# The MLPs' inner activations: transposed by transposing DMA transfers of 16-bit halves instead of by TensorE

## The chip, the cores and the metric

The kernel runs on one core of a Trainium2 chip. The metric is the time of one execution on the device, in microseconds (us); the median of three runs of the kernel before is 2459.45 us (2459.42 to 2463.46).

## The reference

A decoder trunk of two layers for 256 tokens with 2048 features, all in float32. Layer 0 is a retention layer, layer 1 multi-head latent attention; each is followed by an MLP with a squared ReLU and an inner width of 8192:

```
def sq_relu_mlp(h, w1, w2):
    return jnp.square(jax.nn.relu(h @ w1)) @ w2
...
for layer in range(DEPTH):
    ...
    x = x + sq_relu_mlp(rms_norm(x, norm_mlp[layer]), mlp_w1[layer], mlp_w2[layer])
```

The change concerns what happens between the two products of each MLP.

## The kernel before, in words

Activations stand on 128 partitions. A product needs its left operand with the features on the partitions (feature-major), and gives its result with the tokens on the partitions (token-major), 128 tokens in each of two tiles. So the result of `h @ w1` has to be turned before it can be the left operand of the product with `w2`.

Float32 precision is made of three products of a reduced format: each operand is split into a high part and a low part (`split`, line 213: ScalarE casts the high part, VectorE subtracts it for the low part), and `mm` (line 405) issues high times high, high times low and low times high.

**Weights.** `quad` (line 321) takes a megabyte of weights, issued from SP's queue into one of three `raw` buffers, and splits it into high and low parts (`wh`, `wl`, five buffers each). A plain quad has 8 block products, 24 matmuls. In a "seven" quad sums of weight blocks are formed by VectorE first (lines 363 to 373), and 7 block products, 21 matmuls, are enough. `gemm_pair` (line 386) runs eight quads over 1024 result columns and gathers them in four to eight PSUM banks; `pair_out` (line 427) copies the banks out with ScalarE and VectorE combines the sevens' results.

**The MLP.** `mlp` (line 864) goes in four groups. A group has two pieces of `h @ w1` (here u_0 and u_1, named after the count of the piece, p) and two pieces of the product with `w2` (d_00 and d_01: group and piece). Quad k of piece u_1 is u_1k, of piece d_00 it is d_00k. So in each of the two layers four groups of four pieces of eight quads follow each other.

**Between the products.** When a piece u_p has ended, `up` (line 871) runs inside the next piece: it finishes the sums, applies the ReLU with the scale of the norm (ScalarE, line 877), and calls `turn` twice. Each `turn` (line 879) handles 512 columns: for two blocks of 256 columns TensorE transposes four tiles of 128x128 into a PSUM bank (`transposed`, line 230, matmul against the identity at line 235), ScalarE squares from PSUM into SBUF (line 886), `split_act` splits the result, and for the odd blocks `with_sums` (line 451) prepares the sums that sevens need. A piece d_g0 takes its blocks in order: d_004 to d_007 need what u_1 gave, which is turned during d_000 to d_003.

**Order.** Nothing runs ahead of its place in an engine's queue: each engine executes in order. The program is written quad by quad; work between the products is put off by `later` (line 97), which counts in quads, and `tick` runs what is due. A scheduler then merges the work into each engine's queue, so that the order on an engine is not quite the order of the text. Temporaries come from one pool (`f2k`, 14 buffers).

## Time and profile before

| | |
|---|---|
| median of three runs | 2459.45 us |
| span of the profiled execution | 2456.3 us |
| TensorE (PE) busy | 2446.2 us |
| VectorE (DVE) busy | 2212.2 us |
| ScalarE (ACT) busy | 1641.3 us |
| first matmul of the first MLP (u_0), first of d_00 | 721.3 us, 808.6 us from the start |
| last matmul of the second MLP | about 2451 us |
| transposes of the inner activations | 256, 272 ns each |

The time that the profiled execution itself took is not listed beside its span; the medians stand for it. In the rows, PE is TensorE, DVE VectorE, ACT ScalarE, POOL GpSimd and SPq the queue of SyncE, which issues the transfers of weights. A row of the timeline gives the start, the time, the engine, the line, the operation, what it writes and reads, and in brackets the idle time before it and what ended it. "x3" joins instructions in a row, whose times then overlap. Layer numbers and buffer numbers are cut from the names (u_wh, d_raw, hid_u). In the chain of waits a piece is the time from one release to the next.

### The profile page before, as it was taken

To read this page: it belongs to the slowest core of one execution; us is meant where nothing else is said; L and a number is where in the kernel's file an instruction comes from. 1 tells how busy PE (TensorE), PEld (TensorE's weight loads), DVE (VectorE), ACT (ScalarE), POOL (GpSimd) and SP (SyncE) were. 2 spreads that over 40 slices of the span, in tenths; PEclk is the share of its full clock that TensorE was granted. 3 is DMA by queue.
4 is the path that set the end of the run, shared out by engine and by line. 5 is a ranking of instruction groups with operands and counts; after the bars stand their busy time and mean duration, and the time that the engine had idled before them with its cause. 6 is when DMAs were issued, how large, how long until landed. Compare 5 with 4: busy or idle time off the path is not lost.

```text
span 2456.3 us, 31721 instructions
## 1 busy us (share of the span) xinstructions
PE 2446.2 (100%) x11614; PEld 2057.6 (84%) x11614; DVE 2212.2 (90%) x2919; ACT 1641.3 (67%) x2307; POOL 238.0 (10%) x287
## 2 busy tenths in 40 slices
PE   9999999999999999999999999999999999999999
PEld 7888888888888888888888888998888888888887
DVE  7899899888899999999999998777899999999998
ACT  6566666556676767667676777577667667676674
POOL 6400001000000010010110001101000100100100
PEclk9999999999999999999999999999999999999999
DMA  8555569556565586695786555444555865957854
GB/s 309 207 201 191 192 202 259 191 183 224 197 218 194 196 254 218 207 272 187 241 253 213 200 202 180 155 162 173 197 199 205 252 228 194 262 198 229 264 209 170
DMA packets 93692, 521.05 MB, mean 212 GB/s; under 512 B 11104, under 2 KB 12512, under 8 KB 40288
## 3 DMA queue, kind: packets, MB, share of 16 engines
q1 hardware_dynamic: 72144, 472.83, 55.2%
q0 software_dynamic: 21248, 46.15, 8.9%
q8 instruction: 91, 1.49, 0.2%
q14 instruction: 65, 0.53, 0.1%
q10 hardware_dynamic: 144, 0.05, 0.0%
HBM read 479.14 MB, written 39.85 MB: 211 GB/s over the span
## 4 chain that ended last, share of the span: by engine, by line
PE 92%; DVE 2%; ACT 1%; issue 0%; DMA 0%; POOL 0%; ACTq 0%; DVEq 0%
PE u_c L411 7%; PE u_c L410 7%; PE u_c L409 7%; PE d_c L411 6%; PE d_c L410 6%; PE d_c L409 6%; PE rp_c L411 3%; PE rp_c L409 3%; PE rp_c L410 3%; PE u_p L411 2%; PE u_p L410 2%; PE u_p L409 2%; PE rq_acc L307 2%; PE rk_acc L307 2%; PE ro_c L411 2%; PE ro_c L409 2%
## 5 line engine op out<-in xcount | busy, mean ns | idle before, releaser
L217 DVE TENSOR_TENSOR d_wl<-d_raw,d_wh 128x1024 fp32r<-128x1024 f32 (+1 forms) x256 | 278.7, 1111 | 31.6 <-ACT d_wh L216 31.6
L217 DVE TENSOR_TENSOR u_wl<-u_raw,u_wh 128x1024 fp32r<-128x1024 f32 (+1 forms) x256 | 279.3, 1113 | 29.8 <-ACT u_wh L216 29.8
L409 PE MATMUL u_c<-u_wh,n 128*128 128x512 f32 x712 | 278.3, 392 | 0.0
L411 PE MATMUL u_c<-u_wh,n 128*128 128x512 f32 x712 | 277.2, 389 | 0.0
L410 PE MATMUL u_c<-u_wl,n 128*128 128x512 f32 x712 | 277.2, 389 | 0.0
L409 PE MATMUL d_c<-d_wh,hid 128*128 128x512 f32 x706 | 275.4, 392 | 0.5 <-ACT d_wh L216 0.5
L411 PE MATMUL d_c<-d_wh,hid 128*128 128x512 f32 x706 | 275.0, 390 | 0.0
L410 PE MATMUL d_c<-d_wl,hid 128*128 128x512 f32 x706 | 274.8, 389 | 0.0
L216 ACT CAST u_wh<-u_raw 128x1024 fp32r<-128x1024 f32 (+1 forms) x256 | 241.3, 973 | 49.6 <-PE u_c L411 24.1
L216 ACT CAST d_wh<-d_raw 128x1024 fp32r<-128x1024 f32 (+1 forms) x256 | 240.3, 971 | 39.9 <-PE d_c L411 16.6
L216 ACT CAST d_wh<-d_u 128x1024 fp32r<-128x1024 f32 x106 | 108.1, 1051 | 119.7 <-DVE d_u L373 82.6
L216 ACT CAST u_wh<-u_u 128x1024 fp32r<-128x1024 f32 x104 | 106.2, 1052 | 116.0 <-DVE u_u L373 77.3
L411 PEld LDWEIGHTS u_c<-u_wh,n 128*128 128x128 f32 x712 | 133.7, 188 | 27.8
L410 PEld LDWEIGHTS u_c<-u_wl,n 128*128 128x128 f32 x712 | 133.8, 188 | 27.4 <-DVE u_wl L217 0.3
L409 PEld LDWEIGHTS u_c<-u_wh,n 128*128 128x128 f32 x712 | 133.7, 188 | 27.0
L409 PEld LDWEIGHTS d_c<-d_wh,hid 128*128 128x128 f32 x706 | 132.6, 188 | 28.2 <-ACT d_wh L216 1.4
L411 PEld LDWEIGHTS d_c<-d_wh,hid 128*128 128x128 f32 x706 | 132.5, 188 | 27.6
L410 PEld LDWEIGHTS d_c<-d_wl,hid 128*128 128x128 f32 x706 | 132.6, 188 | 27.5 <-DVE d_wl L217 0.4
L216 ACT CAST rp_wh<-rp_raw 128x1024 fp32r<-128x1024 f32 x112 | 103.8, 945 | 74.2 <-PE rp_c L411 49.2
L217 DVE TENSOR_TENSOR rp_wl<-rp_raw,rp_wh 128x1024 fp32r<-128x1024 f32 x112 | 119.7, 1090 | 16.4 <-ACT rp_wh L216 16.2
L217 DVE TENSOR_TENSOR u_wl<-u_u,u_wh 128x1024 fp32r<-128x1024 f32 x104 | 123.5, 1222 | 3.1 <-ACT u_wh L216 2.8
L217 DVE TENSOR_TENSOR d_wl<-d_u,d_wh 128x1024 fp32r<-128x1024 f32 x106 | 125.8, 1221 | 0.0
(570 smaller groups left out, 6505.3 us busy)
## 6 DMA issues: line engine op xcount, KB each, us to landing
u_raw<-in_mlp_w SPq DMA_DIRECT2D x128, 1024.0 KB, 5.4
d_raw<-in_mlp_w SPq DMA_DIRECT2D x128, 1024.0 KB, 4.9
rp_raw<-in_ret_w_gv SPq DMA_DIRECT2D x56, 1024.0 KB, 4.8
ro_raw<-in_ret_w_out SPq DMA_DIRECT2D x32, 1024.0 KB, 4.9
uq_raw<-in_mla_w_uq SPq DMA_DIRECT2D x24, 768.0 KB, 4.3
rq_raw<-in_ret_w_qk SPq DMA_DIRECT2D x16, 1024.0 KB, 4.9
rk_raw<-in_ret_w_qk SPq DMA_DIRECT2D x16, 1024.0 KB, 4.8
xh<-d_c POOLq DMA_DIRECT2D x48, 256.0 KB, 6.1
```

What stands on the lines that cost most here:

```text
L216: nc.scalar.copy(h, src)
L217: return nc.vector.tensor_tensor(l, src, h.bitcast(F32), op=ALU.subtract)
L307: nc.tensor.matmul(acc[f], wh[:, cols], a.rearrange("p i s -> p (i s)"), start=k == 0, stop=k == nk - 1)
L409: nc.tensor.matmul(dst, ah, bh, start=n == 0, stop=False)
L410: nc.tensor.matmul(dst, ah, bl, start=False, stop=False)
L411: nc.tensor.matmul(dst, al, bh, start=False, stop=n == total[key] - 1)
```

## The change

The transposes of `turn` leave TensorE. A float32 word is seen as two 16-bit halves (`halves_of`). After the ReLU, ScalarE copies each tile of 512 columns into two planes, one with the first and one with the second halves (`turn_by_dma`, two copies of 1024 halves for the two token tiles). Two or three quads later SP issues four transposing transfers, one for each token tile and plane, from SBUF to SBUF, 128 partitions x 512 halves (128 KB) each. Then ScalarE joins the planes: for each block of 256 columns it copies the two turned planes of 512 halves into the alternate halves of `u` (`joined`), squares `u` in place, and goes on as before with `split_act` and `with_sums`. The transposing transfers stand in the same queue as the weights' loads.

```diff
+    def halves_of(v):
+        return v.bitcast(U16).rearrange("p (n two) -> p two n", two=2)
+
+    def turn_by_dma(blocks, name, wait, steps, then):
+
+        parts = [f2k([2, 512], f"{name}_h{t}", U16) for t in range(NT)]
+        for t in range(NT):
+            nc.scalar.copy(parts[t], halves_of(blocks[t]))
+
+        def turn():
+            turned = [f2k([4, S], f"{name}_t{i}", U16) for i in range(2)]
+            for t in range(NT):
+                for i in range(2):
+                    nc.sync.dma_start_transpose(turned[i][:, :, t * P : (t + 1) * P], parts[t][:, i])
+            for k2 in range(2):
+                later(steps[k2], lambda k2=k2: then(turned, k2))
+
+        later(wait, turn)
+
+    def joined(turned, k2, u):
+
+        for i in range(2):
+            dst = halves_of(u.rearrange("p j s -> p (j s)"))[:, i]
+            nc.scalar.copy(dst, turned[i][:, 2 * k2 : 2 * k2 + 2].rearrange("p j s -> p (j s)"))
...
                 c = summed(c)
-                for t in range(NT):
-                    for i in range(2):
+
+                def turn(i):
+                    for t in range(NT):
                         nc.scalar.activation(c[t][i], c[t][i], AF.Relu, scale=r[t])
-
-                def turn(i):
-                    for q in (2 * i, 2 * i + 1):
-                        name = f"hid{layer}_{p}{q}"
-                        tp = transposed(
-                            lambda t, j: c[t][q // 2][:, (q % 2 * 2 + j) * P : (q % 2 * 2 + j + 1) * P], f"{name}_tp"
-                        )
-                        u = f2k([2, S], f"{name}_u")
-                        nc.scalar.activation(u, tp, AF.Square)
-                        v = act_tile(name)
-                        split_act(v, u)
-                        blocks.append((v, with_sums(u, name) if len(blocks) in ODD else None))
-                        hid.append(v)
+                    wait = 3 if p % 2 == 0 or i else 2
+                    turn_by_dma(
+                        [c[t][i] for t in range(NT)], f"hid{layer}_{p}{i}", wait, (0, 1),
+                        lambda turned, k2: square(turned, i, k2),
+                    )
+
+                def square(turned, i, k2):
+                    name = f"hid{layer}_{p}{2 * i + k2}"
+                    u = f2k([2, S], f"{name}_u")
+                    joined(turned, k2, u)
+                    nc.scalar.activation(u, u, AF.Square)
+                    v = act_tile(name)
+                    split_act(v, u)
+                    blocks.append((v, with_sums(u, name) if len(blocks) in ODD else None))
```

How the change moves instructions is shown at three places, all at the beginning of piece d_00. The lines of the changed kernel are numbered higher (L213 to L217 became L214 to L218, L363 became L389, L455 became L481).

On VectorE, as d_00 begins: the low parts of its first weights (d_000_wl, d_001_wl) and the sums of piece u_1 (u_1_c, u_1_v, u_1_u, u_1_p). Before:

```order
L217 TENSOR_TENSOR d_000_wl_7401<-d_000_raw,d_000_wh_7400 128x1024
L217 TENSOR_TENSOR d_000_wl_7421<-d_000_raw,d_000_wh_7420 128x1024
L448 TENSOR_TENSOR u_1_c_7386<-u_1_c_7386,u_1_p_7390 128x512
L434 TENSOR_TENSOR u_1_v<-u_1_p_7211,u_1_p_7390 128x512
L435 TENSOR_TENSOR u_1_u<-u_1_p_7211,u_1_v 128x512
L217 TENSOR_TENSOR d_001_wl_7476<-d_001_raw,d_001_wh_7475 128x1024
L438 TENSOR_TENSOR u_1_v<-u_1_p_7392,u_1_v 128x512
L448 TENSOR_TENSOR u_1_c_7388<-u_1_c_7388,u_1_u 128x512
```

And now:

```order
L218 TENSOR_TENSOR d_000_wl_7409<-d_000_raw,d_000_wh_7408 128x1024
L474 TENSOR_TENSOR u_1_c_7394<-u_1_c_7394,u_1_p_7398 128x512
L460 TENSOR_TENSOR u_1_v<-u_1_p_7165,u_1_p_7398 128x512
L461 TENSOR_TENSOR u_1_u<-u_1_p_7165,u_1_v 128x512
L218 TENSOR_TENSOR d_000_wl_7429<-d_000_raw,d_000_wh_7428 128x1024
L464 TENSOR_TENSOR u_1_v<-u_1_p_7400,u_1_v 128x512
L474 TENSOR_TENSOR u_1_c_7396<-u_1_c_7396,u_1_u 128x512
L465 TENSOR_TENSOR u_1_p_7400<-u_1_p_7400,u_1_u 128x512
L474 TENSOR_TENSOR u_1_c_7392<-u_1_c_7392,u_1_v 128x512
L474 TENSOR_TENSOR u_1_c_7390<-u_1_c_7390,u_1_p_7400 128x512
L218 TENSOR_TENSOR d_001_wl_7459<-d_001_raw,d_001_wh_7458 128x1024
```

The second low part of d_000 has moved behind three of the sums, and the first low part of d_001 behind all eight.

On ScalarE, from quad d_003 to quad d_004, now: casts of weights (d_003_wh, d_004_wh), and the joins (L262) of the turned planes (hid_10_t) into hid_10_u and hid_11_u. Before, the casts of d_003 and d_004 follow each other with one cast of hid_13_more between them.

```order
L217 CAST d_003_wh_7579<-d_003_u_7545 128x1024
L262 COPY hid_10_u<-hid_10_t_7530 128x512
L262 COPY hid_10_u<-hid_10_t_7531 128x512
L262 COPY hid_11_u<-hid_10_t_7530 128x512
L915 ACTIVATE hid_10_u<-hid_10_u 128x512
L262 COPY hid_11_u<-hid_10_t_7531 128x512
L217 CAST hid_10_7540<-hid_10_u 128x2x256
L915 ACTIVATE hid_11_u<-hid_11_u 128x512
L217 CAST d_004_wh_7606<-d_004_raw 128x1024
```

The work on the first two blocks of u_1 now stands directly ahead of the first cast of d_004, whose matmuls are the first that need them.

On SP's queue, now, from the load of d_004 on (hid_10_h are the planes, hid_10_t what the transfers write):

```order
L350 DMA d_004_raw<-in_mlp_w_0 128x2048
L252 DMA_TRANSPOSE hid_10_t_7530<-hid_10_h_7452 128x4x128
L252 DMA_TRANSPOSE hid_10_t_7531<-hid_10_h_7452 128x4x128
L252 DMA_TRANSPOSE hid_10_t_7530<-hid_10_h_7453 128x4x128
L252 DMA_TRANSPOSE hid_10_t_7531<-hid_10_h_7453 128x4x128
L350 DMA d_005_raw<-in_mlp_w_0 128x2048
L350 DMA d_006_raw<-in_mlp_w_0 128x2048
L252 DMA_TRANSPOSE hid_11_t_7638<-hid_11_h_7492 128x4x128
```

Before, the loads of d_004 to d_007 follow each other there. Now the first four transfers stand between the loads of d_004 and d_005, and the other four between those of d_006 and d_007.

More of the change, by code (lines that the diff above doesn't have):

```diff
@@ L15 @@
 I32 = mybir.dt.int32
+U16 = mybir.dt.uint16
 AF = mybir.ActivationFunctionType
```

4 lines of the change are left out of this document (2 added, 2 removed).

## The prediction

> **What bounds the kernel now.** The page's first part and its chain of waits come first.
>
> ```profile
> span 2456.3 us, 31721 instructions
> PE 2446.2 (100%) x11614; PEld 2057.6 (84%) x11614; DVE 2212.2 (90%) x2919; ACT 1641.3 (67%) x2307; POOL 238.0 (10%) x287
> ...
> PE 92%; DVE 2%; ACT 1%; issue 0%; DMA 0%; POOL 0%; ACTq 0%; DVEq 0%
> ```
>
> TensorE works in all of the span, and the chain runs through it for 92%. So whatever leaves TensorE's queue is a gain until another engine is late. Which one is next is read by stage: busy time in four stretches of the first MLP (u_1, d_00, d_01 and the stretch after).
>
> ```profile
> core 0: us, PE busy (x) PEld busy (x) DVE busy (x) ACT busy (x) POOL busy (x), PEclk, DMA share, GB/s
> 765.00:808.00 43.00, 43.00 (x200) 35.77 (x199) 40.65 (x52) 31.32 (x43) 0.00 (x0) 1.00 0.57 196
> 808.00:852.00 44.00, 44.00 (x204) 36.62 (x203) 41.86 (x53) 32.31 (x45) 0.00 (x0) 1.00 0.55 192
> 852.00:895.00 43.00, 43.00 (x192) 35.61 (x191) 39.69 (x45) 27.29 (x33) 7.82 (x9) 1.00 0.87 248
> 895.00:938.00 43.00, 43.00 (x191) 35.65 (x190) 39.22 (x44) 28.13 (x33) 6.03 (x7) 1.00 0.91 265
> ```
>
> The first two stretches hold the transposes; VectorE is busy there for 40.65 of 43 and 41.86 of 44 us, about 95%, ScalarE for 73%, and the clock is granted in full. What VectorE does not change, TensorE cannot outrun by much. In the last two VectorE has 92%: there a lag can be worked off.
>
> **What is removed.** The view of a tile gives the number of transposes, the chain in order of time what a run of eight costs, and the timeline TensorE's step.
>
> ```profile
> L235 PE MATMUL hid_tp<-cst,u_c x256: 270/272/273, 770.8 to 2378.3; 128*128 128x128 f32 x128
> ```
> ```profile
> 770.95 0.87 PE hid_tp L235 x8
> ...
> 814.23 0.87 PE hid_tp L235 x8
> ```
> ```profile
> 803.87 0.39 PE L409 MATMUL u_p<-u_wh,n 128*128 128x512 f32 x1
> ...
> 808.17 0.39 PE L410 MATMUL u_p<-u_wl,n_more 128*128 128x512 f32 x1
> ```
>
> One transpose lasts 272 ns, but they overlap: eight take 0.87 us of the chain. 256 of them are 32 runs, so 32 x 0.87 = 27.8 us leave TensorE. That is the ceiling: 2459.45 - 27.8 = 2431.6 us. (The execution shown has a span of 2456.3 us; the 3.1 us up to the median of the runs lie outside what the change touches, so differences are taken from the median.) A matmul of 512 columns starts 0.2265 us after the one before (19 steps in 4.30 us); a quad of 24 takes 5.44 us, a seven of 21 takes 4.76.
>
> **What ScalarE gains in work.** Rows of its timeline in u_1 and at the start of d_00:
>
> ```profile
> 765.55 1.09 ACT L216 CAST u_wh<-u_raw 128x1024 fp32r<-128x1024 f32 x1
> ```
> ```profile
> 804.07 0.59 ACT L432 COPY u_c<-u_c 128x512 f32<-128x512 f32 x1 [1.61 <-PE u_c L411]
> 804.55 1.05 ACT L216 CAST d_wh<-d_raw 128x1024 fp32r<-128x1024 f32 x1
> ...
> 806.93 1.08 ACT L432 COPY u_c<-u_c 128x512 f32<-128x512 f32 x2
> ...
> 810.41 2.98 ACT L216 CAST d_wh<-d_raw 128x1024 fp32r<-128x1024 f32 x3
> 813.24 2.22 ACT L877 ACTIVATE u_c<-u_c,n_r 128x512 f32<-128x512 f32 x3
> ```
>
> Queued behind each other, 1024 elements take 0.95 us, a copy of 512 takes 0.48, a Relu 0.63 (overlapped starts). Each turn adds two copies of 1024 halves and four joins of 512: 2 x 0.95 + 4 x 0.48 = 3.8 us; the Square stays. Two turns fall into a stretch such as 765 to 808: 31.3 + 7.6 = 38.9 us of the 41.3 that TensorE would then need. It fits, if a copy of every second half costs what a plain copy does. No row shows one. From below nothing, since elements are counted alike; from above twice, since it touches every second word.
>
> **What the queue of SP gains.** 128 transposing transfers of 128 KB, eight per pair of turns. No row shows one. The nearest are plain transfers, in the view of the DMA queues and issues, in SP's timeline and in its waits:
>
> ```profile
> q1 hardware_dynamic: 72144, 472.83, 55.2%
> q0 software_dynamic: 21248, 46.15, 8.9%
> ```
> ```profile
> d_raw<-in_mlp_w SPq DMA_DIRECT2D x128, 1024.0 KB, 4.9
> ...
> dec<-in_decay SPq DMA_DIRECT2D x8, 128.0 KB, 4.9
> ...
> x0t<-in_xt SPq DMA_DIRECT2D x2, 128.0 KB, 2.9
> ```
> ```profile
> 772.58 0.33 SPq L324 DMA_DIRECT2D u_raw<-in_mlp_w  x1
> ```
> ```profile
> 815.85 0.33 SPq L324 DMA_DIRECT2D d_raw<-in_mlp_w  x1
> ```
> ```profile
> 819.90 0.33 SPq L324 DMA_DIRECT2D d_raw<-in_mlp_w  x1
> ```
> ```profile
> SPq L324 <- DVE d_wl L217: 592.7, 122, 7.6
> ```
>
> On SP's queue a megabyte keeps the 16 engines for 55.2% of 2456.3 / 472.83 = 2.87 us, on GpSimd's smaller pieces for 4.74; for 128 KB (0.131 MB) that is 0.38 to 0.62 us in a stream. The far end is 2.9 us, a 128 KB transfer alone from issue to landing, if the four of a turn go one after another. I take 0.5, between the two queues, because the four stand in one queue behind a load like a stream. Engines have the room: eight are 4 us, and in 43 us they are idle for 43%. SP itself issues a plain transfer in 0.33 us and otherwise waits for VectorE to let go of raw buffers (122 waits, 592.7 us). In the new order four transfers stand behind d_004's load; what is queued behind them is d_005's load, whose buffer is free only 4 us after d_004's (815.85 and 819.90). So they delay no load if each is issued within 1 us.
>
> [...]
>
> **Where it is late.** I follow one pair of turns by hand, on the clock of the profile; VectorE's rows carry it.
>
> ```profile
> 801.51 2.35 DVE L217 TENSOR_TENSOR u_wl<-u_u,u_wh 128x1024 fp32r<-128x1024 f32 x2
> ```
> ```profile
> 805.63 1.23 DVE L217 TENSOR_TENSOR d_wl<-d_raw,d_wh 128x1024 fp32r<-128x1024 f32 x1 [1.76 <-ACT d_wh L216]
> ...
> 811.60 0.69 DVE L438 TENSOR_TENSOR u_v<-u_p,u_v 128x512 f32<-128x512 f32 x1
> 812.20 0.68 DVE L448 TENSOR_TENSOR u_c<-u_c,u_u 128x512 f32<-128x512 f32 x1
> ...
> 814.60 2.36 DVE L217 TENSOR_TENSOR d_wl<-d_raw,d_wh 128x1024 fp32r<-128x1024 f32 x2
> 816.87 0.42 DVE L455 TENSOR_TENSOR hid_sum<-hid_u 128x256 f32<-128x256 f32 x1
> ...
> 818.41 0.29 DVE L456 TENSOR_TENSOR hid_sum<-hid_sum,hid_u 128x128 f32<-128x128 f32 x1
> 818.61 1.22 DVE L217 TENSOR_TENSOR d_wl<-d_raw,d_wh 128x1024 fp32r<-128x1024 f32 x1
> ```
>
> In a queue, 1024 elements take VectorE 1.13 us (the last of a run 1.23), 512 take 0.60, 256 take 0.34, 128 take 0.20.
>
> In u_1, the load of u_14 issues at 772.6 and lands 4.9 later, the four transfers at about 779.6. ScalarE has by then run up against the first join: from u_11's first cast at 765.55 it has ten items of 1024 (that one, five casts, four copies of halves), four Relus and one item of 512 queued, 765.55 + 9.5 + 2.5 + 0.5 = 778.1. So 1.5 us are lost; then join, cast of u_13, join, Square, join, hid cast, cast of u_14: 779.6 + 0.95 + 5 x 0.48 + 1.06 = 784.0, and VectorE's low part of u_14 ends at 785.1. From there to u_17's first low part its queue holds eight passes of 1024 and the last of 1.23, ten of 512, two of 256 and four of 128: 9.04 + 1.23 + 6.0 + 0.68 + 0.8 = 17.7 us, so 802.8. TensorE, two runs (1.74) earlier than 803.87, asks for it at its second matmul, 802.13 + 0.23 = 802.4. **Late: about 0.5 us.**
>
> In d_00 TensorE then starts at 802.13 + 0.5 + 4.76 = 807.4. ScalarE casts u_17's sums, which VectorE ends at 801.7, until 803.8; four copies and a cast later its copy of p1 ends at 807.2, and three sums of VectorE at 809.05. By the new order d_000's second low part follows (810.2), five sums (813.2) and only then d_001's first low part: 814.4. TensorE wants it at 807.4 + 5.44 + 0.23 = 813.1. **Late: 1.3 us.** With that TensorE is back at its old clock (d_001 at 814.1; d_004 at 829.8). d_004's load issues when d_001's low part is done, 815.5, lands at 820.4, the four transfers at 822.4. ScalarE reaches the first join at 823.6 (there are five high-part buffers, and the cast before takes the one that TensorE uses until 822.7): no wait, 1.2 us to spare. Seven items of 0.48 and a cast later, at 828.1, d_004's cast is done, its low part at 829.3, in time for 830.0. From there to d_006's first low part VectorE has five passes of 1024, the last of 1.23, seven of 512 and one of 256 queued, 11.4 us: 840.7, wanted at 839.97 + 0.23 = 840.2. **Late: 0.5**, and to d_007's another 5.7 us (two of 1024, one of 1.23, three of 512, two of 128), 846.4, wanted at 846.1: **late 0.3**.
>
> **The sum.** A group of four pieces has two turns in u_1 and two in d_00: 4 x 0.87 = 3.5 us off, 0.5 + 1.3 + 0.5 + 0.3 = 2.6 back, 0.9 kept. Two layers of four groups: 8 x 0.9 = 7 us. 2459.45 - 7 = **2452 us**. An error of 1 us in a group is 8 us in the time; the forecast's own range is 2444 to 2461.
>
> **The rivals.**
>
> *All of it is kept.* The low parts are in time, as VectorE's lead of about 3 us (it ends u_17's low parts at 803.9, TensorE uses the last from 807.3) swallows the lateness. For it: no stretch exceeds VectorE's time. Against it: 95% busy there, and VectorE idle 1.76 us at the head of each piece for ScalarE, which waits for TensorE. 2432 to 2444 us, say 2437.
>
> *The transfers land after their joins (slower).* The place is d_00: ScalarE is in order, so a join that waits holds up the weights' casts behind it, and with them VectorE and TensorE. Above 0.5 + 1.2 / 4 = 0.8 us per transfer the joins of d_00 wait; each of the 16 transfers of a group then costs what it has above 0.8. The 0.9 us kept are gone at 0.86 us per transfer: from there on it is slower. At 1.0 us it loses 16 x 0.2 = 3.2 us a group, 8 x 3.2 = 26 in all: 2478 us. For it: both queues' packets are longer than the rows of a transpose, and 0.8 is near to 0.62.
>
> *Each transfer waits for the one before.* At 2.9 us, 16 x 2.1 x 8 = 269 us: 2721 us. Against it: loads of one queue overlap in these rows. [...]
>
> *ScalarE's half copies cost twice.* Then 31.3 + 15.2 = 46.5 us against 41.5 in 16 stretches: 5 x 16 = 80, 2532 us. Against it: a cast and a copy take ScalarE equally long per element in the rows.
>
> **The numbers.** A measurement of this kernel tells a difference of about 0.2% (5 us) from none. Forecast 0.43 (0.28 of it below 2454.5, 0.15 within); all kept 0.20; late landing 0.27 (0.04 within); one after another 0.05; double copies 0.05. So faster 0.48, same 0.19, slower 0.33. The range leaves out the last two and the tail of late landings above 1.05 us, and the best of the second: 2433 to 2486.
>
> **What the profile would show.** Right: no hid_tp rows, a PE span shorter by 5 to 10 us; idle time of PE before d_c and u_c that ends with VectorE's low part, 2 to 3 us in a group; ScalarE at about 73%; joins that wait little for the transfers. If TensorE has no such idle time, all is kept; if ScalarE's joins wait for DMA, the transfers are late; if L246 and L262 take twice 0.95 and 0.48, the copies are the cost. Wrong in its ground would be a TensorE that waits for raw weights, since I let the transfers delay no load.

## The result and the profile after

| | median us | change |
|---|---|---|
| before | 2459.43 | |
| after | 2501.12 (2500.70 to 2503.62) | ratio 1.0167 [1.0153, 1.0181] |

It is slower by 41.7 us. The forecast was 2452, faster, in a range of 2433 to 2486: the sign was wrong and the time lies outside the range. The profiled execution of after took 2501.51 us. The head of its page, its chain and its queue:

```profile
span 2499.7 us, 31622 instructions
PE 2447.4 (98%) x11358; PEld 2023.3 (81%) x11358; DVE 2219.1 (89%) x2919; ACT 1765.5 (71%) x2499; POOL 239.5 (10%) x287
...
q1 hardware_dynamic: 141776, 489.62, 59.6%
...
PE 64%; DVE 15%; ACT 10%; DMA 5%; issue 4%; SPq 1%; POOL 0%; ACTq 0%; DVEq 0%
```

The 256 transposes are gone from TensorE, but a third of the chain now runs through other engines. What TensorE waits for is in its waits (total us, times, longest):

```profile
PE d_c L435 <- ACT d_wh L217: 14.4, 17, 2.9
PE d_c L436 <- DVE d_wl L218: 10.5, 17, 1.5
PE u_c L436 <- DVE u_wl L218: 8.5, 10, 0.9
PE u_p L436 <- DVE u_wl L218: 3.6, 11, 0.6
PE d_p L436 <- DVE d_wl L218: 2.6, 8, 0.3
...
PE u_c L435 <- ACT u_wh L217: 1.5, 2, 0.7
```

These are 41.1 us in 65 waits; before, d_c had 0.5 and the others no row. Its timeline shows that a wait costs more than its bracket:

```profile
795.85 0.40 PE L435 MATMUL u_c<-u_wh,n 128*128 128x512 f32 x1
797.12 0.50 PE L436 MATMUL u_c<-u_wl,n 128*128 128x512 f32 x1 [0.87 <-DVE u_wl L218]
797.46 0.40 PE L437 MATMUL u_c<-u_wh,n 128*128 128x512 f32 x1
...
806.17 0.50 PE L436 MATMUL u_p<-u_wl,n 128*128 128x512 f32 x1 [0.36 <-DVE u_wl L218]
...
817.82 0.50 PE L436 MATMUL d_c<-d_wl,hid 128*128 128x512 f32 x1 [0.66 <-DVE d_wl L218]
...
839.02 0.50 PE L436 MATMUL d_p<-d_wl,hid 128*128 128x512 f32 x1 [0.33 <-DVE d_wl L218]
...
852.14 0.50 PE L435 MATMUL d_c<-d_wh,hid 128*128 128x512 f32 x1 [0.45 <-ACT d_wh L217]
...
863.98 0.50 PE L435 MATMUL d_c<-d_wh,hid 128*128 128x512 f32 x1 [0.96 <-ACT d_wh L217]
```

Counted by matmuls from the start of a pair (a plain quad has 24, a seven 21), these six waits are in quads u_15, u_17, d_001, d_005, d_007 and, already in d_01, d_011. The step to 797.12 is 1.27 us instead of 0.2265, 1.04 late where the bracket says 0.87, and the next step is 0.34. So each wait costs some 0.27 more: 41.1 + 65 x 0.27 = 58.7, less the 27.8 removed, is an estimate of 31 of the 41.7 us. The rest lies in longer steps without a row of their own.

**Where it sits.** The starts of the pieces give it by pairs, from the first matmul of one pair to that of the next (before: 84.08 us a pair, 87.3 for the first of a layer). The eight pairs of u together take 9.95 us longer. So do, by 20.94, the six pairs of d that a pair of u follows directly; the last pair of d of each layer, read with the stage behind it, adds 6.9 and 3.8, and 1.8 lie ahead of the first MLP. All below is told in the first two sums, "u" and "d".

**Why TensorE waits** is read on the engines that feed it. VectorE's waits after, and those of the same kind before:

```profile
DVE u_wl L218 <- ACT u_wh L217: 51.2, 45, 4.5
DVE hid L218 <- ACT hid L217: 37.7, 25, 3.5
...
DVE d_wl L218 <- ACT d_wh L217: 7.2, 14, 0.7
```
```profile
DVE u_wl L217 <- ACT u_wh L216: 32.7, 30, 1.8
DVE d_wl L217 <- ACT d_wh L216: 31.6, 28, 1.8
```
```profile
L217 DVE TENSOR_TENSOR hid<-hid_u,hid 128x512 fp32r<-128x512 f32 x64 | 41.4, 690 | 0.0
```

The three kinds are 96.1 us against 64.3 (hid had none before, as its group in the third fence shows: busy time, mean of one, idle time). VectorE, 95% busy in these pieces before, does not get back what it loses: by the page its busy time rose by 6.9 us and its idle time by 36.5, which is the whole 43.4 by which the span grew. It waits for ScalarE, and this is what ScalarE does there:

```profile
781.52 0.77 ACT L262 COPY hid_u<-hid_t 128x512 uint16<-128x512 uint16 x1 [1.19 <-DMA hid_t<-hid_h]
...
826.40 2.03 ACT L262 COPY hid_u<-hid_t 128x512 uint16<-128x512 uint16 x3
828.30 0.62 ACT L915 ACTIVATE hid_u<-hid_u 128x512 f32<-128x512 f32 x1
828.83 0.75 ACT L262 COPY hid_u<-hid_t 128x512 uint16<-128x512 uint16 x1
829.45 0.61 ACT L217 CAST hid<-hid_u 128x512 fp32r<-128x512 f32 x1
...
836.08 1.41 ACT L262 COPY hid_u<-hid_t 128x512 uint16<-128x512 uint16 x2 [1.62 <-DMA hid_t<-hid_h]
```
```profile
830.09 0.69 DVE L218 TENSOR_TENSOR hid<-hid_u,hid 128x512 fp32r<-128x512 f32 x1 [2.32 <-ACT hid L217]
```

Two things are to be seen. At 826.40 nothing waits for a transfer: three joins, a Square, a join and a cast stand behind each other, and VectorE (second fence) is idle for 2.32 us until the cast is done. At 781.52 and 836.08 ScalarE itself is idle, for a transfer that has not landed. The first is order, the second lateness, and the experiments take them apart.

### The profile page after: what moved, and what is told of

It is laid out like the page before. It is cut to its first block, busy times and chain, and to the rows that moved or that the text cites. A ratio compares the mean times of both kernels' runs of the same rounds, so it can differ in the third digit from the quotient of the medians.

```text
span 2499.7 us, 31622 instructions
## 1 busy us (share of the span) xinstructions
PE 2447.4 (98%) x11358; PEld 2023.3 (81%) x11358; DVE 2219.1 (89%) x2919; ACT 1765.5 (71%) x2499; POOL 239.5 (10%) x287
## 3 DMA queue, kind: packets, MB, share of 16 engines
q1 hardware_dynamic: 141776, 489.62, 59.6%
## 4 chain that ended last, share of the span: by engine, by line
PE 64%; DVE 15%; ACT 10%; DMA 5%; issue 4%; SPq 1%; POOL 0%; ACTq 0%; DVEq 0%
PE u_c L436 4%; PE u_c L437 4%; PE u_c L435 4%; DVE d_wl L218 4%; DMA hid_t<-hid_h 3%; PE d_c L436 3%; PE d_c L437 3%; PE d_c L435 3%; PE rp_c L435 2%; PE rp_c L437 2%; PE rp_c L436 2%; PE rq_acc L333 2%; PE rk_acc L333 2%; ACT u_wh L217 2%; DVE u_wl L218 2%
## 5 line engine op out<-in xcount | busy, mean ns | idle before, releaser
L218 DVE TENSOR_TENSOR u_wl<-u_raw,u_wh 128x1024 fp32r<-128x1024 f32 (+1 forms) x256 | 277.4, 1110 | 31.5 <-ACT u_wh L217 30.8
L218 DVE TENSOR_TENSOR d_wl<-d_raw,d_wh 128x1024 fp32r<-128x1024 f32 (+1 forms) x256 | 276.4, 1107 | 6.6 <-ACT d_wh L217 6.2
L437 PE MATMUL d_c<-d_wh,hid 128*128 128x512 f32 x706 | 275.4, 390 | 0.0
L435 PE MATMUL d_c<-d_wh,hid 128*128 128x512 f32 x706 | 259.8, 392 | 14.4 <-ACT d_wh L217 14.4
L217 ACT CAST u_wh<-u_raw 128x1024 fp32r<-128x1024 f32 (+1 forms) x256 | 242.8, 971 | 37.8 <-PE u_c L437 18.0
L217 ACT CAST d_wh<-d_raw 128x1024 fp32r<-128x1024 f32 (+1 forms) x256 | 238.2, 972 | 26.5 <-DMA d_raw<-in_mlp_w 15.8
L217 ACT CAST d_wh<-d_u 128x1024 fp32r<-128x1024 f32 x106 | 107.4, 1051 | 107.7 <-DVE d_u L399 82.8
L217 ACT CAST u_wh<-u_u 128x1024 fp32r<-128x1024 f32 x104 | 106.8, 1050 | 88.0 <-DVE u_u L399 59.5
L217 ACT CAST rp_wh<-rp_raw 128x1024 fp32r<-128x1024 f32 x112 | 103.8, 944 | 74.6 <-PE rp_c L437 49.7
L218 DVE TENSOR_TENSOR u_wl<-u_u,u_wh 128x1024 fp32r<-128x1024 f32 x104 | 123.2, 1218 | 20.7 <-ACT u_wh L217 20.4
L218 DVE TENSOR_TENSOR rp_wl<-rp_raw,rp_wh 128x1024 fp32r<-128x1024 f32 x112 | 119.3, 1086 | 16.9 <-ACT rp_wh L217 16.8
L218 DVE TENSOR_TENSOR d_wl<-d_u,d_wh 128x1024 fp32r<-128x1024 f32 x106 | 124.8, 1217 | 1.1 <-ACT d_wh L217 1.0
```

Source lines behind the costliest of these rows:

```text
L217: nc.scalar.copy(h, src)
L218: return nc.vector.tensor_tensor(l, src, h.bitcast(F32), op=ALU.subtract)
L435: nc.tensor.matmul(dst, ah, bh, start=n == 0, stop=False)
L437: nc.tensor.matmul(dst, al, bh, start=False, stop=n == total[key] - 1)
```

## The experiments

The expectations call the explanations by letters. Theory A: the transfers land late because of their own price, as the rival in the prediction had it. Rival B: ScalarE's added copies and the new order are the loss, whatever the transfers do. Rival C: the order alone that the scheduler laid out around the transfers is the loss. Theory D: what costs is the transfers' place in a queue, behind a weight load and ahead of the next, whatever their price.

All times, with the 95% interval of the ratio to before and the two sums (changes in us against before). A sum is read from the profiled execution, whose own time is up to 3.7 us from the median:

| kernel | us | ratio | u | d |
|---|---|---|---|---|
| after | 2501.12 | [1.0153, 1.0181] | +9.95 | +20.94 |
| no_transfer | 2452.69 | [0.9957, 0.9980] | -9.35 | -1.57 |
| plain | 2472.08 | [1.0033, 1.0063] | -0.74 | +5.44 |
| tensor_plus_transfers | 2459.93 | [0.9987, 1.0006] | 0 | 0 |
| even_by_dma | 2471.38 | [1.0032, 1.0062] | +6.63 | +2.02 |
| no_transfer_order | 2473.75 | [1.0042, 1.0076] | -7.86 | +14.10 |
| plain_order | 2497.50 | [1.0139, 1.0169] | +12.37 | +17.74 |
| plain_rows_order | 2496.09 | [1.0136, 1.0166] | +9.44 | +19.21 |
| early_transfers | 2500.54 | [1.0153, 1.0184] | +29.77 | +5.96 |
| nt_order_ahead | 2467.89 | [1.0022, 1.0046] | +5.43 | -0.44 |
| ahead_order | 2489.42 | [1.0106, 1.0137] | +7.54 | +13.92 |
| even_queued_12 | 2490.32 | [1.0109, 1.0143] | +23.47 | +4.63 |
| even_queued_sp | 2469.19 | [1.0024, 1.0046] | +1.09 | +4.68 |
| full_order | 2471.98 | [1.0034, 1.0063] | -3.47 | +9.33 |
| tensor_same_places | 2459.46 | [0.9988, 1.0007] | 0 | 0 |
| plain_pool_order | 2477.44 | [1.0057, 1.0087] | -5.51 | +14.08 |
| no_transfer_pool | 2489.47 | [1.0102, 1.0136] | +8.94 | +13.16 |
| pool_joins | 2513.27 | [1.0206, 1.0237] | +17.25 | +22.87 |
| after_d1 | 2501.24 | [1.0151, 1.0179] | +12.20 | +22.64 |

### Taking the transfers away, and adding them where nobody waits

no_transfer: the transfers go, the joins read the half copies.

```diff
-                    nc.sync.dma_start_transpose(turned[i][:, :, t * P : (t + 1) * P], parts[t][:, i])
...
-            nc.scalar.copy(dst, turned[i][:, 2 * k2 : 2 * k2 + 2].rearrange("p j s -> p (j s)"))
+            nc.scalar.copy(dst, turned[k2][:, i])
```

> No transfers at all: the joins read the half copies directly (the turning is left out). ScalarE keeps all of its added work. Theory A: nothing is late but what ScalarE and VectorE make late themselves, so 2437 to 2455 us, not above the kernel with plain transfers. Rival B: 2490 to 2500 us, since ScalarE has the same 16 copies per pair of turns.

tensor_plus_transfers: before, with 128 transposing transfers that nobody reads.

```diff
+                def extra(i):
...
+                            nc.sync.dma_start_transpose(
+                                turned[h][:, :, t * P : (t + 1) * P],
+                                c[t][i].bitcast(U16)[:, h * 512 : (h + 1) * 512],
+                            )
...
+                    later(3 if p % 2 == 0 or i else 2, lambda: extra(i))
```

> The kernel before, with TensorE's transposes kept, and the 128 transposing transfers added at the places they have in the changed kernel; nobody reads what they write (the output is as before). No instruction of ScalarE, VectorE or TensorE is added or moved. Theory A splits: what the transfers do by holding SP (a weight load behind them issued up to 5 us later) shows here, without the joins that wait: 2465 to 2490 us if the late loads are the larger half of the loss, 2459 to 2465 if the late joins are. Rival B: 2459 us, as before.

plain: the same pieces moved without turning.

```diff
-                    nc.sync.dma_start_transpose(turned[i][:, :, t * P : (t + 1) * P], parts[t][:, i])
+                    nc.sync.dma_start(turned[i][:, :, t * P : (t + 1) * P], parts[t][:, i].rearrange("p (j n) -> p j n", j=4))
```

> Each transposing transfer of the changed kernel is replaced by a plain transfer of the same 128 KB between the same tiles on the same queue (the activations stay unturned: that part of the computation is left out). Theory A (the price of the transposing transfers: SP held 1.31 us by each, 1.05 us of the 16 engines' time, joins and weight loads late behind them): SP is held about 0.33 us per transfer, the joins no longer wait, and the time falls from 2501 to what was forecast blind, 2444 to 2461 us. Rival B (ScalarE's added copies and the new order on VectorE cost it, whatever the transfers do): it stays at 2490 to 2501 us.

even_by_dma: only the first piece of a pair is turned by transfers, the second by TensorE as before.

```diff
                 def turn(i):
+                    if p % 2 == 1:
+                        return by_tensor(i)
```

> Only the first piece of each pair, whose turns run beside the second u piece, is turned by transfers; the second, whose turns run beside the first d piece, by TensorE as before. 16 runs of TensorE's transposes leave, 13.9 us. In the changed kernel the u pairs took about as long as before, with their 1.74 us each given back, and the d pairs lost 3.4 us. Theory A: so no loss is left and a part of the 13.9 us may stay: 2452 to 2462 us. Rival B: half of ScalarE's added work stays, half the loss: about 2480 us.

Without transfers the time is 2452.69, with ScalarE's added work in it, and the pairs are 1.2 (u) and 0.3 us (d) shorter. So ScalarE's copies by themselves are not the loss; rival B asked for 2490 to 2500 here. That the time is the forecast's own number is chance, for the forecast had transfers in it. With transfers that nobody reads, nothing is lost, although two loads stand behind eight of them, as SP's timeline shows:

```profile
773.84 4.41 SPq L325 DMA_DIRECT2D u_raw<-in_mlp_w  x2
778.31 10.65 SPq L884 DMA_TRANSPOSE x_t<-u_c  x8
789.06 1.09 SPq L325 DMA_DIRECT2D u_raw<-in_mlp_w  x2
```

The last two loads are issued from 789.06 on, where before all four were out in one run from 772.58 to 788.89. So neither the engines' time nor a late load alone is the price, while ScalarE and VectorE keep their old work. plain in its own order is 29 us faster than after, but the scheduler gave it another order, so that this comparison has two causes in it; at 2472.08 it lies between the two ranges expected, and so does even_by_dma. even_by_dma, half of the change, is 11.9 us slower than before, so there too the cost is more than the half of 27.8 that it takes off.

### Holding the order

In the kernels named "_order" the order of after (or the one named) is fixed on ScalarE, VectorE and TensorE, and where said on SP, by a chain over each engine's own instructions (their lines are numbered 22 or more higher):

```diff
+        for a, b in zip(order, order[1:]):
+            tc.add_manual_dep(
+                own[b], own[a].name,
+                mybir.DependencyInfo(mybir.DependencyClass.NoSync, mybir.DependencyReason.DATA), reason="order",
+            )
```

no_transfer_order is the edit of no_transfer in after's order, plain_order that of plain. plain_rows_order moves 512-byte pieces:

```diff
-                    nc.sync.dma_start_transpose(turned[i][:, :, t * P : (t + 1) * P], parts[t][:, i])
+                    row = turned[i].rearrange("p j s -> p (j s)").rearrange("p (k u n) -> p k u n", k=2, u=NT)
+                    nc.sync.dma_start(row[:, :, t], parts[t][:, i].rearrange("p (k n) -> p k n", k=2))
```

> No transfers (the joins read the half copies, the turning is left out), and every instruction of ScalarE, VectorE and TensorE held in the order that the changed kernel has; the kernel without transfers before this one had an order of its own. Theory A, now without its late loads (the joins wait for transfers that land late, and ScalarE holds its casts up meanwhile): without transfers this order costs what the other did, 2450 to 2457 us. Rival C (not the transfers but the order that the scheduler laid out around them costs it): 2475 to 2500 us.

> The kernel with plain transfers in pieces of 256 bytes, held in the order of the changed kernel on every engine, SP's too: what it differs in from the changed kernel is the price of the transposing alone. Theory A: as in its own order, 2465 to 2480 us, since a transfer holds SP 0.75 to 1.0 us and not 1.31 and lands sooner. Rival C: 2490 to 2501 us, the transfers' price is no matter.

> As the one before, with pieces of 512 bytes instead of 256 (half as many), the same tiles, bytes and dependencies, the changed kernel's order. Theory A: the price of a transfer goes with its pieces, so it lands sooner again and SP is held 0.4 to 0.6 us: 2455 to 2470 us, below the kernel with 256-byte pieces by 5 us or more. If the price goes with the bytes, the two are equal. Rival C: 2490 to 2501 us.

early_transfers lets the transfers start two quads earlier, their joins where they were:

```diff
-                        [c[t][i] for t in range(NT)], f"hid{layer}_{p}{i}", wait, (0, 1),
+                        [c[t][i] for t in range(NT)], f"hid{layer}_{p}{i}", wait - 2, (2, 3),
```

> The changed kernel with its transposing transfers written two quads earlier and the joins at the quads where they were (so the transfers have two quads, 10 us, more; they go ahead of more weight loads in SP's queue; the scheduler lays the rest out anew). Theory A: the joins find their data, and the time falls towards the kernel without transfers: 2453 to 2465 us. If the late weight loads behind the transfers were the cost (already against the run with TensorE's transposes kept): 2490 us or above. Rival C gives no number, since the order is another.

Without a single transfer after's order takes 2473.75, 21.1 us more than no_transfer in its own: far above theory A's range and just under rival C's. By the sums, 15.7 of it are in d and 1.5 in u. VectorE's waits in no_transfer_order and its group in no_transfer differ in one kind above all:

```profile
DVE hid L240 <- ACT hid L239: 28.3, 16, 2.3
```
```profile
L218 DVE TENSOR_TENSOR hid<-hid_u,hid 128x512 fp32r<-128x512 f32 x64 | 43.9, 685 | 3.6 <-ACT hid L217 3.6
```

The idle time at hid goes from 3.6 to 28.3 us, 16 times with up to 2.3: by the timeline once in each pair of u with 1.25 (behind the first join, at 783.7) and once in each pair of d with 2.3 (at 828.0). The second is the bunch at 826.40, and no transfer is in it. Rival C holds for this part. Where TensorE pays for it is seen in no_transfer_order's own rows: from start to start, the six pairs of d are late by 0.49 us in d_005, 0.5 in d_007 and 1.13 to 1.16 in d_011 (the row below), and none of the three is in no_transfer.

```profile
860.20 0.50 PE L453 MATMUL d_c<-d_wh,hid 128*128 128x512 f32 x1 [0.96 <-ACT d_wh L239]
```

The wait of u_15 (797.12 in after) is not in no_transfer_order. There the first join of the turn waits for no transfer; in after it is 1.19 us late (781.52), the cast behind it is late with it, and VectorE stands idle for that cast:

```profile
783.23 1.23 DVE L218 TENSOR_TENSOR u_wl<-u_u,u_wh 128x1024 fp32r<-128x1024 f32 x1 [1.17 <-ACT u_wh L217]
```

That idle time is not in no_transfer_order either. So u_15 is late by the transfers, and the three of d by the order.

With plain transfers in the same order the time is 2496.09 (512 bytes) or 2497.50 (256 bytes): 22 to 24 us more, and only 4 to 5 us below after. Transposing is then a small part. By the sums of plain_rows_order and no_transfer_order, the transfers cost 17.3 us in u and 5.1 in d. What one transfer costs, from the views of the tile (SP's hold of one: least, median, most in ns) of after, plain_order and plain_rows_order:

```profile
L252 SPq DMA_TRANSPOSE hid_t<-hid_h x128: 1194/1306/2975, 775.2 to 2426.2; - x128
```
```profile
L274 SPq DMA_DIRECT2D hid_t<-hid_h x128: 593/696/3064, 775.2 to 2420.3; - x128
```
```profile
L275 SPq DMA_DIRECT2D hid_t<-hid_h x128: 593/624/2019, 775.3 to 2419.5; - x128
```

The engines' time, from q1's share (59.6% of 2499.7 = 1489.8 us, less 1355.9 before, by 128), is 1.05 us per transposing transfer; by the same sum it is 0.76 for 256-byte and 0.60 for 512-byte pieces. At 0.60, below the 0.8 us from which the prediction's rival lets the joins wait, the loss is almost the same. So theory A falls. early_transfers takes as long as after, in other places: d is better by 15.0 and u worse by 19.8. Eight transfers now stand ahead of the loads of u (10.54 us of SP's queue from 775.27 on), and ScalarE's casts of u wait 28.3 us for raw weights, where after has 4.1. The joins still wait 17.6 us, and the mean granted clock of its profile is 0.996, after's 0.999, so that a part of its time may be clock.

### Another place in SP's queue, or another queue

ahead_order is after with each four transfers ahead of the load that they follow. nt_order_ahead has the transfers of after in no_transfer's order, ahead of the load as well. In even_queued_12 only the first piece is turned by transfers and its joins are put a quad later, behind a high-part cast:

```diff
-            nc.scalar.copy(h, src)
+            high_part[0] = nc.scalar.copy(h, src)
...
+            queued_behind(ins, high_part[0])
...
-                        [c[t][i] for t in range(NT)], f"hid{layer}_{p}{i}", wait, (0, 1),
+                        [c[t][i] for t in range(NT)], f"hid{layer}_{p}{i}", wait, (1, 2),
```

> The changed kernel, its order of ScalarE, VectorE and TensorE held as it is; on SP's queue alone each four transfers of a turn are moved ahead of the megabyte weight load that they stood behind. Theory D (what costs is the time from half copy to join, in which the transfers stand in one queue behind a weight load; their own price is small): the first join of a turn finds its data, and the time comes near the run without transfers in this order, 2474 to 2485 us. If instead the transfers' own price is what the joins wait for, or the load that is now behind them: 2495 us or more.

> The changed kernel, with its transfers ahead of the loads on SP's queue as in the run before, and ScalarE, VectorE and TensorE held in the order that the kernel without transfers had (joins spread between the casts, earlier than in the changed kernel). If the order is all that differs between 2453 and 2474 us: 2455 to 2465 us. If the transfers, though ahead of the loads, land later than this order asks for them, ScalarE waits at the joins by 2 us or more in most of the 32 turns: 2490 us or more.

> Only the first piece of a pair is turned by transfers (in the second u piece, whose outcome nobody needs before the next piece), and its joins are held back on ScalarE behind the casts of the quad being made, one quad later than in the changed kernel; the second piece by TensorE as before. Without waits and without a deadline a u pair should take what it takes without transfers, 82.9 to 83.2 us against 84.08 before, a d pair 84.1 as before: 8 x 1.0 less, 2450 to 2454 us, the first version faster than the kernel before with real transfers. If ScalarE's and VectorE's added work is late wherever it stands: 2460 us or more, as the run with the first piece alone (2471).

even_queued_sp is the same with the transfers held behind u_15's load. full_order has all pieces turned, the first piece of a pair that way, d's transfers ahead of their load, in the order of a twin without transfers. tensor_same_places is tensor_plus_transfers with the transfers at after's places in SP's queue.

> The run with the first piece alone turned by transfers and its joins a quad later (2490 us), every instruction of ScalarE, VectorE and TensorE in the order it had there; on SP's queue alone the eight transfers of a u pair stand behind u_15's load and not ahead of it. If it was the late load of u_15 that made that run slow (ScalarE waited 33.1 us for raw u weights there): 2450 to 2458 us, 32 us or more off, and faster than the kernel before. If it was the late joins: 2480 us or more.

> All turns by transposing transfers, as in the changed kernel, with both cures: in the u pieces the transfers behind u_15's load and the joins a quad later, in the d pieces the transfers ahead of the loads of d_004 and d_006; ScalarE, VectorE and TensorE in the order that this kernel has when the joins need no transfers. If waits at joins and late loads are all that the transfers cost: u pairs 83 us, d pairs 83.9, 2450 to 2458 us. If the price of a transfer, 1.05 us of the engines' time and 1.31 us of SP's, costs wherever it stands: 2475 us or more.

> The kernel before with TensorE's transposes and the 128 transposing transfers added, as an earlier run, but on SP's queue each four at exactly the place they have in the changed kernel (behind the loads of u_14 and u_15, of d_004 and d_006). There they stood behind u_15's load, all eight of a pair, and cost nothing. What this adds over the kernel before is the price of the late weight loads alone, since nobody waits for the transfers. If loads late by 4 to 5 us at these places are swallowed by the three raw buffers: 2458 to 2462 us. If they are a part of the changed kernel's loss: 2468 us or more, and ScalarE's waits for raw weights grow by 10 us or more.

SP's queue of even_queued_12 and ScalarE's waits for raw weights in even_queued_12 and in ahead_order:

```profile
773.68 10.50 SPq L252 DMA_TRANSPOSE hid_t<-hid_h  x8
784.28 1.92 SPq L353 DMA_DIRECT2D u_raw<-in_mlp_w  x3
```
```profile
ACT u_wh L217 <- DMA u_raw<-in_mlp_w: 33.1, 13, 5.3
```
```profile
ACT u_wh L239 <- DMA u_raw<-in_mlp_w: 20.0, 13, 2.5
```

Eight transfers hold SP for 10.50 us, and the next load is out at 784.28. So even_queued_12, meant for 2450 to 2454, takes 2490. Moved behind one load more, the same transfers cost 21 us less (2490.32 and 2469.19; the ten runs of the second lie from 2464.2 to 2473.9). In ahead_order the joins wait no more (0.4 us in all) and d is better by 7.0 us and u by 2.4, while the casts of u wait 20.0 us for raw weights where after has 4.1. Theory D has its shape: in one queue either the joins or the raw weights are late, and moving the transfers trades one for the other. tensor_same_places, with the same places as after, loses nothing, although its casts of u and d wait 17.8 us for raw weights where before has 11.4. This suggests, and no run shows, that a late load is paid only where ScalarE and VectorE have no slack left for it. The best with real transfers for all pieces is nt_order_ahead, 2467.89, 15.2 more than no_transfer; full_order is not better. Nearly all of the 15.2 is in u, where VectorE's sums of raw weights wait 20.3 us for them, against 10.6 in no_transfer. ahead_order, nt_order_ahead, even_queued_sp and full_order all came out between the ranges expected: no place in SP's queue gave all of it back.

plain_pool_order is plain_rows_order with the transfers issued by GpSimd:

```diff
-                    nc.sync.dma_start(row[:, :, t], parts[t][:, i].rearrange("p (k n) -> p k n", k=2))
+                    nc.gpsimd.dma_start(row[:, :, t], parts[t][:, i].rearrange("p (k n) -> p k n", k=2))
```

> The kernel with plain transfers in pieces of 512 bytes (2496 us from SP's queue; the activations stay unturned), ScalarE, VectorE and TensorE in the changed kernel's order, the transfers issued by GpSimd on its own queue instead of SP's. Nothing stands ahead of them there and no weight load behind them. Theory D (they land late because they queue behind a megabyte of weights): the joins no longer wait, near the run without transfers in this order, 2474 to 2484 us. If a transfer's own way, from half copies to the landing, is what the joins wait for: 2490 us or more.

2477.44 against 2496.09: of the 22.3 us that plain transfers cost in after's order 18.7 go when they leave SP's queue. The timelines of SP in plain_rows_order and of GpSimd in plain_pool_order show why:

```profile
774.53 0.33 SPq L373 DMA_DIRECT2D u_raw<-in_mlp_w  x1
775.33 2.77 SPq L275 DMA_DIRECT2D hid_t<-hid_h  x4
```
```profile
770.88 1.49 POOL L275 DMA_DIRECT2D hid_t<-hid_h  x2 [33.84 <-DMA u_raw<-in_mlp_w]
774.33 1.44 POOL L275 DMA_DIRECT2D hid_t<-hid_h  x2 [1.96 <-ACT hid_h L268]
```
```profile
L285 ACT COPY hid_u<-hid_t 128x512 uint16<-128x512 uint16 x128 | 92.9, 769 | 1.9 <-DMA hid_t<-hid_h 1.9
```

On GpSimd the first two transfers are out as soon as their half copies are made, at 770.88; on SP they stand behind a load that gets its buffer at 774.53, and go out from 775.33 on. The larger step is at the second turn of d_00: there its four transfers are out from 819.02 on GpSimd and from 825.84 on SP. The joins (third fence, plain_pool_order) wait 1.9 us in all instead of 23.2, and the loads of u follow each other without transfers between. Landing itself took hardly less, 5.7 us in the median against 6.2. How much of the 18.7 is the earlier start and how much the loads' was not taken apart. Transposing transfers on that queue weren't tried.

### The joins on GpSimd, and a piece of the order

no_transfer_pool and pool_joins are no_transfer and after with the joins on GpSimd, each in an order of the scheduler's own. The line of pool_joins:

```diff
-            nc.scalar.copy(dst, turned[i][:, 2 * k2 : 2 * k2 + 2].rearrange("p j s -> p (j s)"))
+            nc.gpsimd.tensor_copy(dst, turned[i][:, 2 * k2 : 2 * k2 + 2].rearrange("p j s -> p (j s)"))
```

> No transfers (the turning is left out), and the joins are made by GpSimd, not by ScalarE, in an order of the scheduler's own. It asks where the 21 us stay that the kernel without transfers (2452.7) still lacks of 2431.6. If it is ScalarE's eight joins per pair of turns (6.2 us of each 43): 2436 to 2446 us. If it is VectorE, which has no more work than before but a shorter time for it: 2450 to 2456 us. If GpSimd beside VectorE slows VectorE's passes: above 2456 us.

> The changed kernel with its transposing transfers, the joins made by GpSimd, in an order of the scheduler's own. ScalarE then waits at the Square of a turn and not at the join, GpSimd's copy standing between transfer and Square. Theory D: the wait is longer by that copy and only its place changes: 2490 us or more. If ScalarE's joins were the cost: 2480 us or less.

Both are slower than their partners, by 36.8 and 12.2 us. The join takes longer there (1389 ns in no_transfer_pool instead of 779 in no_transfer), and VectorE's subtractions beside it do too (groups of no_transfer_pool, then the subtraction in no_transfer):

```profile
L258 POOL COPY hid_u<-hid_h 128x512 uint16<-128x512 uint16 x128 | 169.6, 1389 | 385.0 <-ACT hid_h L246 385.0
```
```profile
L218 DVE TENSOR_TENSOR d_wl<-d_raw,d_wh 128x1024 fp32r<-128x1024 f32 x203 | 255.0, 1272 | 1.8 <-ACT d_wh L217 1.8
```
```profile
L218 DVE TENSOR_TENSOR d_wl<-d_raw,d_wh 128x1024 fp32r<-128x1024 f32 x203 | 244.8, 1220 | 11.2 <-ACT d_wh L217 11.0
```

1272 instead of 1220 ns in the mean, 4% more, on the engine that is about 95% busy in no_transfer too. One by one, the 30 of these subtractions that run beside a copy of GpSimd take 1590 ns in the mean, the other 173 take 1217. How much of the 36.8 us this is, and how much the longer join, was not taken apart; so the question that no_transfer_pool was to answer, where the 21.1 us between 2431.6 and 2452.7 stay, is open. In pool_joins the granted clock falls to 0.5 for 3.4 us 13 times, in after once (0.991 against 0.999 in the mean), and its 12.2 us may be in part that.

after_d1 is after with the eight VectorE passes at the start of d_01 put back, in six groups, to the order of before; nothing else moves.

> The changed kernel, every engine held in its order but for eight passes of VectorE at the start of the second d piece of six groups: the sums of d_011's raw weights go back ahead of the outcome sums of d_00, as they stood before the change. Transfers and joins are as in the changed kernel. There TensorE stood 1.13 us for a high part that ScalarE casts from these sums. If that order alone is the cause, 6 x 1.13 = 6.8 us come off: about 2494 us, d pairs shorter by about 1.1 us each, u pairs as they were. If the wait there comes from the late joins of the piece before: no change, 2499 to 2502 us.

2501.24: no change. TensorE's wait moved from the high part (863.98 in after, [0.96]) to a high and a low part:

```profile
862.62 0.50 PE L457 MATMUL d_c<-d_wh,hid 128*128 128x512 f32 x1 [0.24 <-ACT d_wh L239]
863.93 0.50 PE L458 MATMUL d_p<-d_wl,hid 128*128 128x512 f32 x1 [0.80 <-DVE d_wl L240]
```

VectorE's work there is late as a whole, and which pass goes first does not matter. So this swap is not the cost of the order. In after's order, the bunches in d_00 are where the idle time sits; that they are the cost is not shown, for undoing them alone was not tried.

**The sum**, in the order in which the steps were taken apart: 27.8 off (2431.6, which no run reached); 21.1 back in no_transfer, with ScalarE's work and an order of its own (2452.7); 21.1 for the order (2473.75); 22.3 for plain transfers in SP's queue (2496.1); 5.0 for turning and smaller pieces (2501.1). Another sequence would give other shares, for the steps share one slack: in no_transfer's order, ahead of the load, the transfers cost 15.2. No kernel here is faster than no_transfer, which doesn't turn, and none that turns everything by transfers is faster than before.

## Why the prediction was wrong, point by point

**ScalarE's work** was nearly right; the ceiling no run reached. The joins take 0.63 queued (three in 2.03 us with 0.77 for the last) instead of 0.48, the half copies 1071 ns, about what a cast of 1024 elements takes (1062); ScalarE's busy time rose by 124.2 us against 32 x 3.8 = 121.6. With joins of 0.63 the same sum is 141, so that the nearness is in part luck. The rival of double half copies is out. A pair, by forecast 1.24 us shorter in u and 0.36 longer in d, came out at -1.17 and -0.26 in no_transfer, which has no transfers and another order.

**The transfer's price** was mis-sized, 0.5 against 1.05 us of the engines' time and 1.31 us of SP's; the condition for "they delay no load", issue within 1 us, is not met. Four in a row held SP for 5.25 us together (775.16 to 780.41). From issue to landing a transfer took 5.0 us in the median, and a plain one in the same place (plain_order) 6.0. But the price is not what decided: 0.60 us lost nearly as much in the same place.

**The step that failed is "Where it is late".** I followed one chain of work and asked for the low parts of five quads only. Of these, d_004 was in time as foretold (in four of six pairs), u_17 came late as foretold (0.52 us from start to start for 0.5) and d_001 with less (0.82 for 1.3); d_006 had no wait of its own (0.5 foretold), and d_007 one of 0.61 (0.3), for a high part of ScalarE. That is 2.0 for 2.6, and luck in its parts. What I put at nothing, without having asked, are three other quads: u_15 with 1.04 us, d_005 with 0.49 and more, d_011 with 1.13. u_15 comes from the late first join: I had its 1.5 us of ScalarE's time, but carried them to u_17 alone, past u_15. d_005 and d_011 come with the order, also without transfers. I counted VectorE's items as queued without a gap, where it stands idle for 2.3 us at the bunch of 826.40, which I had shown in the order without asking who waits for its last item. So a pair of u, 1.24 us shorter by forecast, became 1.24 longer, and a pair of d, 0.36 longer by forecast, became 3.5 longer.

**"In the last two a lag can be worked off"** was wrong: in d_01 a wait of 1.13 us (863.98) follows. VectorE has 92% there, and what it can make up is only its 8%.

**The rival of late landing** had the right side and the right sign (joins that wait hold up the casts behind them: 27.7 us), by the wrong cause. Its threshold of 0.8 us per transfer plays no part; the place in the queue does, and 21 of the 49 us between forecast and result were order, which no rival named. Its chance, 0.27, was too small for a kernel in which VectorE had 5% left.

**The signs foretold**: waits of TensorE that end with the low parts came, 25.2 us, 3.2 a group for 2 to 3, and with the high parts, which were not foretold, 41.1, 5.1 a group; ScalarE at 71% for 73%; and joins that wait, the sign of the rival. TensorE itself waits for no raw weights.

## What to carry to other kernels

Work taken from the bounding engine is worth only what the next engine has free; where that one is 95% busy, count its idle time, not its work, and ask of every bunch in the order who waits for its last item. Follow every item that the bounding engine asks for, not a few of them: the waits of three quads that I had left out came to more than those that I had counted. A transfer whose data another engine waits for doesn't belong in a queue behind loads that wait for buffers: it is issued when they let it, not when its data is ready (in plain_rows_order at 775.33, for a half copy that ended at 771.10; in plain_pool_order, from GpSimd's queue, at 770.88 for one that ended at 770.59). To tell order from cost, hold the order fixed and leave the operation out.

## What the runs showed of the hardware

A transposing transfer of 128 KB from SBUF to SBUF kept the 16 engines 1.05 us (125 GB/s) and SP 1.31 us in after; the same pieces without turning took 0.76 and 0.70 in plain_order. So with these pieces turning cost 0.29 us more of the engines' time and 0.61 us more of SP's.

Where GpSimd's queue moved data too (29.5% of the 16 engines' time from 1270 to 1310), four transfers took SP still longer, and the join waited; SP's and ScalarE's rows of after in the last pair of u of the first layer:

```profile
1293.28 7.93 SPq L252 DMA_TRANSPOSE hid_t<-hid_h  x4
```
```profile
1302.85 0.78 ACT L262 COPY hid_u<-hid_t 128x512 uint16<-128x512 uint16 x1 [4.03 <-DMA hid_t<-hid_h]
```

Behind that wait TensorE ran eight matmuls with a step of 0.43 us instead of 0.2265, and the granted clock was 0.69 in the stretch:

```profile
1308.00:1313.00 5.00, 4.22 (x11) 3.15 (x12) 5.00 (x7) 5.00 (x8) 0.00 (x0) 0.69 0.96 315
```

This low clock came once in the MLPs of this profile. The long hold and the late join came again in the last pair of u of the second layer (7.57 us, the join waiting 4.56), with the clock in full. What brings them on was not tried.
